# Wider weight pieces, later and earlier statistics, and one-pass transposes in a decoder trunk

## The chip, the cores and the metric

One core of one Trainium2 chip runs the whole program. The metric is device time of one launch in microseconds, the median of several runs; 1053.26 us for the kernel before, from 3 runs (1051.03 to 1053.49).

## The reference, cut to what matters

The input is `h` of 256 tokens x 1024, all in float32. Two layers, each a half-step SwiGLU feed-forward, a token mixer, and another half-step feed-forward; the mixer of the first layer is Mamba-2 (one chunk of 256 tokens, 32 heads in 4 groups), that of the second a sliding-window attention with sinks. A shared K/V projection stands between the layers.

```python
def rmsnorm(x, g):
    y = x * lax.rsqrt(jnp.mean(x * x, axis=-1, keepdims=True) + EPS)
    return y * g

def swiglu_half_step(h, g, w1, w3, w2):          # w1, w3: 1024 x 2816; w2: 2816 x 1024
    u = rmsnorm(h, g)
    return h + 0.5 * ((jax.nn.silu(u @ w1) * (u @ w3)) @ w2)

h = swiglu_half_step(h, ...)                     # layer 0, first FFN
h = h + mamba2_mixer(rmsnorm(h, ssm_norm), ...)  # ends in a grouped rmsnorm of y*silu(z), then @ w_out
h = swiglu_half_step(h, ...)
k, v = shared_kv(h, ...)
h = swiglu_half_step(h, ...)                     # layer 1
h = h + sliding_window_attention(rmsnorm(h, attn_norm), k, v, ...)
return swiglu_half_step(h, ...)                  # the last FFN
```

## The kernel before, in words

The residual stream lives transposed in SBUF: `hT` holds 8 tiles of 128 channels x 256 tokens. A matrix product in float32 is made from three products of float32r parts: a weight is cast to a high part `wh` by ScalarE and the rest `wl` is taken by VectorE (`Unit.part`, lines 165 to 169); activations have a high and a low part likewise (`vh`/`vl` from `Norm.split`, `uT` from `Norm.normalize`). From chunk 2 on (`up_wide`) one 512-column matmul does two of the three products.

**Weights.** A `Unit` (line 146) is 2048 columns of raw weights, fetched by SyncE into one of 3 buffers `raw`, and cut into 4 pieces of 512 columns; each piece is one cast and one subtraction. `wh` and `wl` are buffers of 1024 columns, 8 of each, so two pieces share a buffer and both wait until TensorE has read what was there. The raw buffer comes free, and SyncE issues the next fetch, when its last piece is subtracted.

**A feed-forward** (`run_ffn`, line 303) has 11 chunks of 256 hidden columns in two halves f. Each half is an up-projection (16 weight blocks), a `gate` (silu and product, split into parts) and the down-projection of an earlier half (`flush`). The rms factor does not stop it: the first chunks run on the unnormalised `vh`/`vl`, while `Norm.stats` computes 1/rms (`token_mean`: two float32 matmuls with a 1-column operand; an add on VectorE; a power on GpSimd) and `Norm.scale` spreads it over partitions (`spread`, line 228: two float32 matmuls of a broadcast column with the identity, and a copy). Then `normalize` writes `uT`. When these two steps stand in the instruction order is given as counts of matmuls: `later(n, fn)` runs `fn` once n more matmuls have been written.

**The last feed-forward** yields tokens on partitions, so its residual has to be transposed back: `residual` (line 412) adds `hT.T @ (2*identity)` into the four accumulators by 16 float32 matmuls, and the end multiplies by 0.5.

**Mamba** (`mamba`, line 476). `stage_a0` computes z and dt from unnormalised parts, with statistics and scale at 62 and 100 matmuls; `a_bc`, `a_x`, `a_z` are projections of group g with a convolution on VectorE; `stage_b` makes y of a group and its sum of squares `sq` (line 773); `stage_y(g, 30, 60)` places the group's statistics and its scaling (`y_stats`, `y_scale`) 30 and 60 matmuls later, beside the next group's projections; `stage_c`/`c_part` are the output projection.

**The opening** (lines 1125 to 1183) loads x in two halves (`xin`), transposes it by `turn_x(b)`, two channel tiles at a time, and casts the first weights piece by piece in a pinned order (`chained`, `behind`). `turn_x(2)` and `turn_x(3)` are called ahead of contraction steps 1 and 3 of the first up-projection.

**Order.** Each engine runs its queue in order. The order is laid out when the program is built, by a planner that goes by program order as priority and by its own estimates of what is ready; `tc.issue_after` pins an instruction behind another of its engine, `tc.high_priority` moves it ahead. Inside attention the matmul order is pinned (`strict`).

Of the kernel before, what the change touches and what calls it, by code (L numbers as in the profile page):

```python
# [11 lines left out]
F32 = mybir.dt.float32  # L12
F32R = mybir.dt.float32r
AF = mybir.ActivationFunctionType
ALU = mybir.AluOpType
# [3 lines left out]
P = 128  # L19
D = 1024  # L20
KT = D // P
S = 256
NT = S // P
# [17 lines left out]
def yoco_kernel(ctx: ExitStack, tc: tile.TileContext, a: dict, out: bass.AP):  # L41
    nc = tc.nc
# [11 lines left out]
    def bcast(src: bass.AP, n: int, off: int = 0, parts: int = P) -> bass.AP:  # L54
        return bass.AP(tensor=src.tensor, offset=src.offset + off, ap=[[0, parts], [1, n]])
# [21 lines left out]
    mean = const.tile([P, 2], F32, name="mean")  # L77
    nc.gpsimd.memset(mean[:, 0:1], 1.0 / D)
    nc.gpsimd.memset(mean[:, 1:2], 1.0 / 512.0)
    ident2 = const.tile([P, P], F32, name="ident2")  # L80
    nc.gpsimd.tensor_add(ident2, ident, ident)

    anti = const.tile([P, P], F32, name="anti")
    nc.gpsimd.memset(anti, 0.0)
    nc.gpsimd.affine_select(out=anti, in_=anti, pattern=[[1, P]], compare_op=ALU.not_equal, fill=1.0,
# [8 lines left out]
    def nm(s):  # L94
        uid[0] += 1
        return f"{s}_{uid[0]}"
# [5 lines left out]
    def in_turn(op, *args, **kw):  # L102
        if strict[0]:
            with tc.issue_after(pe[-1]):
                r = op(*args, **kw)  # L105
        else:
            r = op(*args, **kw)  # L107
        pe.append(r.ins)

    def mm(o, l, r, first, last):  # L110
        in_turn(nc.tensor.matmul, o, l, r, start=first, stop=last)
# [15 lines left out]
    def later(n, fn):  # L127
        soon.append((len(pe) + n, fn))
# [11 lines left out]
    def wmm3(o, wh, wl, uh, ul, first, last):  # L140
# [2 lines left out]
        mm(o, wl, uh, False, last)  # L143
        tick()

    class Unit:
        def __init__(self, parts, split=2, hold=False):
            n = 2048 // split
            raw = rawp.tile([P, 2048], F32, tag="raw", name=nm("raw"))
            for part in parts:  # L150
                if callable(part):
                    part()
                    continue
                lo, n0, shape, src, k0 = part
                nc.sync.dma_start(view(raw, shape, lo, n0)[:, k0:k0 + src.shape[1]], src)
            self.h, self.l = [], []
            self.raw, self.n = raw, n
            for i in range(split):
                self.h.append(whp.tile([P, n], F32R, tag="wh", name=nm("wh")))
                self.l.append(wlp.tile([P, n], F32R, tag="wl", name=nm("wl")))  # L160
            if not hold:
                for c in range(0, 2048, 512):
                    self.part(c)

        def part(self, c):
            rs = self.raw[:, c:c + 512]
            wh, wl = self.get(c, 512)
            return (nc.scalar.copy(wh, rs).ins,  # L168
                    nc.vector.tensor_sub(wl, rs, wh.bitcast(F32)).ins)  # L169

# [9 lines left out]
    def up_unit(w1, w3, c, half, cut=1, hold=False, between=None):  # L180
        cs = slice(c * 256, c * 256 + 256)
        n = 4 // cut
        parts = []
        for k in range(0, 4, n):
            r0 = half * 512 + k * P
            for i, w in enumerate((w1, w3)):
                parts.append((i * 256, 256, 512,
                              w[r0:r0 + n * P, cs].rearrange("(k p) c -> p k c", p=P), k))
            if between is not None and k == 0:
                parts.append(between)  # L190
        return Unit(parts, hold=hold)

    def row_unit(w, r0, hold=False):
        return Unit([(0, 1024, 1024, w[r0:r0 + 256, :].rearrange("(k p) c -> p k c", p=P), 0)], hold=hold)
# [33 lines left out]
    def spread(rs):  # L228
        pb = ps_tr.tile([P, S], F32, tag="tr", name=nm("pb"))
        for t in range(NT):  # L230
            mm(pb[:, t * P:(t + 1) * P], rs[:, t:t + 1].to_broadcast([P, P]), ident, True, True)
        rb = sb.tile([P, S], F32, tag="rsb", name=nm("rsb"), bufs=2)
        nc.vector.tensor_copy(rb, pb)
        return rb
# [68 lines left out]
    def run_ffn(layer, j, cur, nxt, hook=None, ups=None, at=(60, 84), pre=None):  # L303
# [5 lines left out]
        last = nxt is None  # L309
# [99 lines left out]
                for d in range(KT):  # L409
                    down(c, f, d, g)  # L410

        def residual():
            for t in range(NT):
                for n in range(2):
                    for i in range(4):
                        mm(acc[2 * t + n][:, i * P:(i + 1) * P], hT[:, 4 * n + i, t * P:(t + 1) * P],
                           ident2, False, False)

        pend = []

# [5 lines left out]
        slow = at[1] > 96  # L426
        for c in range(NCHUNK):
            for f in range(2):
                if c == 0 and f == 0:
                    later(*stats)  # L430
                    later(*scale)
                    with tc.issue_after(pe[-1]) if pe else nullcontext():
                        g0 = up_first()
                    if not slow:
                        start_gates()
                if c == 0:
                    continue
                pm = up(c, f)
                if slow and c == 1 and f == 0:
                    start_gates()  # L440
                g = gate(c, pm)
                if c < C:
                    if not (slow and c == 1 and f == 0):
                        flush(pend.pop(0))
                    if c == 1 and f == 1:
                        while pend:
                            flush(pend.pop(0))
                    pend.append((c, f, g))
                elif f == 0:
                    gc0 = g  # L450
                if c == 5 and len(gcols) == 1:
                    gain_cols(grow[1])
                if c == 5 and f == 0 and last:
                    residual()
                if c >= 3 and hook is not None:
                    next(hook, None)
        pend = pend[0]
# [9 lines left out]
        for t in range(NT):  # L467
            for n in range(2):
                down_t(C, 0, t, n, gc0)
                down_t(C, 1, t, n, g)  # L470
                cs = slice(n * 512, n * 512 + 512)
                o = sb.tile([P, 512], F32, tag="cv", name=nm("o"), bufs=2)
                nc.vector.tensor_scalar_mul(o, acc[2 * t + n], 0.5)
                nc.sync.dma_start(out[0, t * P:(t + 1) * P, cs], o)

    def mamba(mp, cur, nxt):
# [198 lines left out]
        def stage_a0():  # L675
            zs = mp.tile([P, 4, S], F32, tag="zs", name=nm("zs"), bufs=2)
            uz = [col_unit(w_in, [i * 256], 256) for i in range(2)]
            later(62, cur.stats)
            later(100, cur.scale)
            z0 = z_first(uz[0], ps_acc, "acc")  # L680
            dt_proj()
            z1 = z_first(uz[1], ps_mm, "mm")
            dt_scale()
            z_scale(z0, zs[:, 0:2, :])
            cur.normalize()
            z_scale(z1, zs[:, 2:4, :])
            a_bc(0)
            dt_soft()
            a_x(0)
            dt_cum()  # L690
            decay_rows(0)
            st[0] = st[0] + (zs,)
# [116 lines left out]
        def stage_y(g, n0, n1):  # L809
            later(n0, lambda: y_stats(g))  # L810
            later(n1, lambda: y_scale(g))
# [28 lines left out]
        stage_b(0)  # L840
        exps(1)
        for g in (2, 3):
            stage_y(g - 2, 30, 60)
            a_bc(g)
            prep(g - 1)
            a_x(g)
            a_z(g)
            stage_b(g - 1)
            exps(g)
            if g == 2:  # L850
                stage_c(0)
# [80 lines left out]
    def attention(ap, cur, kT, vtok, bias, nxt):  # L932
        snk = ap.tile([P, AH], F32, tag="snk", name="snk")
        nc.gpsimd.dma_start(snk, bcast(a["sinks"][0], AH))
        uq = [row_unit(a["w_q"][0], i * 256) for i in range(4)]
        qns, qTs = {}, {}

# [181 lines left out]
        for b in range(KT // 2):  # L1119
            for d in (2 * b, 2 * b + 1):  # L1120
                for k in range(4, KT):
# [6 lines left out]
    n0.open()  # L1128
    w13 = a["ffn_w1"][0, 0], a["ffn_w3"][0, 0]
    keep_warm(10)  # L1130
    ups = {0: [up_unit(*w13, 0, 0, 2, True,
                       lambda: nc.sync.dma_start(xin[:, :, 512:1024], xsrc[:, :, 512:1024]))]}
    ups[0].append(up_unit(*w13, 0, 1, 2, True))
    ups[1] = [up_unit(*w13, 1, h, 2, True) for h in range(2)]
# [6 lines left out]
    def turn_x(b):  # L1141
        pool, tag = ((ps_tr, "tr"), (ps_acc, "acc"), (ps_acc, "acc"), (ps_mm, "mm"))[b]
        px = pool.tile([P, 2, S], F32, tag=tag, name=nm("px"))
        for i in range(2):
            for t in range(NT):
                nc.tensor.transpose(px[:, i, t * P:(t + 1) * P],
                                    xin[:, t, (2 * b + i) * P:(2 * b + i + 1) * P], ident)
        if b == 0:
            gain_cols(grow[0])
        for i in range(2):  # L1150
            with behind(*(prev[-1] if prev else ())):
                n0.split(2 * b + i, px[:, i, :])
            with behind(*n0.last):
                prev.append(ups[0][b // 2].part((b % 2) * 1024 + i * 512))
        pxs.append(px)

    def keep_x():
# [17 lines left out]
        for b in (3, 0, 1, 2):  # L1175
# [3 lines left out]

    turn_x(0)  # L1180
    turn_x(1)
    run_ffn(0, 0, norms[0], norms[1], ups=ups, at=(128, 142),
            pre={1: lambda: turn_x(2), 3: lambda: turn_x(3), 7: keep_x})
    xpool.close()
    with tc.tile_pool(name="mp", bufs=1) as mp:
        mamba(mp, norms[1], norms[2])
# [45 lines left out]
```

## Time and profile before

| what | value |
|---|---|
| median of 3 runs | 1053.26 us (1051.03 to 1053.49) |
| the profiled execution, own time | 1054.95 us |
| its span, first to last instruction | 1053.2 us |
| mean granted TensorE clock | 0.995 |
| VectorE busy | 760.0 us (72%) |
| ScalarE busy | 628.1 us (60%) |
| DMA moved | 187.22 MB, mean 178 GB/s |

Busy time is the union of an engine's instructions. A matmul's record is longer than the time to the next one's start, since matmuls are pipelined: a row of the timeline that merges n matmuls gives the start of the first and the end of the last, so the pace is read from starts. "PEld" is the weight load of a matmul. The clock is the share of full speed that was granted to TensorE: 1.00 is 2.4 GHz, 0.50 is 1.2 GHz.

### The profile page before, as it was taken

The numbers are of one execution on the slowest core, as the hardware profiler recorded it, in microseconds if no ns is written. First come the engines' busy times: TensorE is split into PE (matmuls) and PEld (weight loads), VectorE is DVE, ScalarE is ACT, GpSimd is POOL, SyncE is SP. The second block draws the span as 40 slices with busy tenths as digits, with TensorE's granted clock in tenths as the row PEclk, the third lists the DMA queues.
The fourth block names the chain that finished last, engine by engine and source line by source line (L and its number), as shares of the span: only waits on it lengthen the run. The fifth ranks groups of instructions, "written<-read, shape, count | busy, mean of one in ns | idle before, by whom it ended". The sixth has DMA issues, their size and how long they took to land.

```text
span 1053.2 us, 18596 instructions
## 1 busy us (share of the span) xinstructions
PE 1037.4 (98%) x7130; PEld 950.7 (90%) x7130; DVE 760.0 (72%) x1564; ACT 628.1 (60%) x1348; POOL 54.5 (5%) x79
## 2 busy tenths in 40 slices
PE   8999999999999999999999999999999999999998
PEld 8999999989899999999999999999986699888886
DVE  6975756897899899756566976675677678564753
ACT  7664655677867656646456754465567566454652
POOL 1100000003210010000000000010002000000000
PEclk9999999999999999999999999999999999999999
DMA  8665657546456365556565556585641336464641
GB/s 287 210 223 172 207 174 215 173 129 204 135 169 225 133 173 192 180 181 203 171 224 160 191 173 200 163 284 173 222 160 41 120 122 212 154 225 129 217 142 41
DMA packets 138921, 187.22 MB, mean 178 GB/s; under 512 B 4940, under 2 KB 120816, under 8 KB 138832
## 3 DMA queue, kind: packets, MB, share of 16 engines
q1 hardware_dynamic: 136496, 179.32, 52.8%
q0 software_dynamic: 2288, 6.69, 2.2%
q8 instruction: 56, 0.92, 0.4%
q14 instruction: 33, 0.27, 0.1%
q10 hardware_dynamic: 48, 0.02, 0.0%
HBM read 184.90 MB, written 1.11 MB: 177 GB/s over the span
## 4 chain that ended last, share of the span: by engine, by line
PE 72%; issue 21%; DVE 4%; POOL 1%; DMA 1%; ACT 1%; SPq 0%; POOLq 0%; DVEq 0%; ACTq 0%
PE pm L107 37%; PE acc L107 18%; PE pa L107 5%; PE pp L107 5%; PE pq L105 2%; PE pa L105 1%; PE ps L105 1%; DVE wl L169 1%; PE py L107 1%; DVE sp L982 1%; PE po L105 1%; DMA xin<-in_x_dram 1%; PE pkv L107 1%; ACT em L607 1%; DVE zs L767 1%
## 5 line engine op out<-in xcount | busy, mean ns | idle before, releaser
L169 DVE TENSOR_TENSOR wl<-raw,wh 128x512 fp32r<-128x512 f32 x676 | 434.5, 685 | 54.0 <-ACT wh L168 41.5
L168 ACT CAST wh<-raw 128x512 fp32r<-128x512 f32 x676 | 375.6, 618 | 84.5 <-PE acc L107 32.1
L107 PE MATMUL pm<-uT,wh 128*128 128x512 f32 x1152 | 402.9, 392 | 0.0
L107 PE MATMUL pm<-uT,wl 128*128 128x256 f32 x1152 | 321.7, 280 | 0.0
L107 PEld LDWEIGHTS pm<-uT,wh 128*128 128x128 f32 x1152 | 216.1, 188 | 45.7 <-issue 0.2
L107 PEld LDWEIGHTS pm<-uT,wl 128*128 128x128 f32 x1152 | 216.5, 188 | 1.1 <-DVE wl L169 0.2
L107 PE MATMUL acc<-ghl,wh 128*128 128x256 f32 x1056 | 191.2, 282 | 0.0
L336 ACT COPY lo<-pm 128x256 f32<-128x256 f32 x144 | 53.3, 370 | 211.0 <-PE pm L107 211.0
L337 DVE TENSOR_TENSOR tp<-pm,lo 128x256 f32<-128x256 f32 x144 | 60.8, 422 | 154.4 <-ACT lo L336 154.4
L107 PEld LDWEIGHTS acc<-ghl,wh 128*128 128x128 f32 x1056 | 162.3, 188 | 2.7 <-ACT ghl L344 0.3
L107 PE MATMUL acc<-ghl,wl 128*128 128x256 f32 x528 | 148.3, 282 | 0.0
L107 PE MATMUL pp<-uT,wh 128*128 128x256 f32 x576 | 107.1, 287 | 2.2 <-ACT uT L300 1.4
L107 PEld LDWEIGHTS acc<-ghl,wl 128*128 128x128 f32 x528 | 99.4, 188 | 0.0
L107 PEld LDWEIGHTS pp<-uT,wh 128*128 128x128 f32 x576 | 90.4, 192 | 3.1 <-ACT uT L300 1.5
L107 PE MATMUL pp<-uT,wl 128*128 128x256 f32 x288 | 81.5, 284 | 0.0
L107 PE MATMUL pm<-vh,wh 128*128 128x256 f32 x256 | 73.2, 286 | 0.0
L107 PE MATMUL pm<-vl,wh 128*128 128x256 f32 x256 | 72.4, 283 | 0.0
L107 PE MATMUL pm<-vh,wl 128*128 128x256 f32 x256 | 72.3, 283 | 0.0
L107 PE MATMUL acc<-wh,ghl 128*128 128x512 f32 x176 | 58.3, 395 | 0.0
L107 PEld LDWEIGHTS pp<-uT,wl 128*128 128x128 f32 x288 | 55.1, 191 | 0.0
L344 ACT CAST ghl<-g 128x256 fp32r<-128x256 f32 x88 | 35.7, 406 | 31.6 <-DVE g L341 31.2
L345 DVE TENSOR_TENSOR ghl<-g,ghl 128x256 fp32r<-128x256 f32 x88 | 36.9, 420 | 17.5 <-ACT ghl L344 17.5
(234 smaller groups left out, 1275.5 us busy)
## 6 DMA issues: line engine op xcount, KB each, us to landing
raw<-in_ffn_w_dram SPq DMA_DIRECT2D x168, 512.0 KB, 4.8
raw<-in_ffn_w_dram SPq DMA_DIRECT2D x44, 1024.0 KB, 5.2
raw<-in_ssm_w_in_dram SPq DMA_DIRECT2D x16, 1024.0 KB, 5.4
raw<-in_ssm_w_out_dram SPq DMA_DIRECT2D x8, 1024.0 KB, 5.0
raw<-in_ffn_w_dram SPq DMA_DIRECT2D x16, 256.0 KB, 6.0
raw<-in_ssm_w_in_dram SPq DMA_DIRECT2D x8, 512.0 KB, 5.3
pr<-pdram POOLq DMA_DIRECT2D x8, 512.0 KB, 4.4
raw<-in_w_q_dram SPq DMA_DIRECT2D x4, 1024.0 KB, 4.9
```

The costliest lines, as they stand in the source:

```text
L105: r = op(*args, **kw)
L107: r = op(*args, **kw)
L168: return (nc.scalar.copy(wh, rs).ins, nc.vector.tensor_sub(wl, rs, wh.bitcast(F32)).ins)
L169: nc.vector.tensor_sub(wl, rs, wh.bitcast(F32)).ins)
L336: nc.scalar.copy(lo, pw[:, 256:512])
L337: nc.vector.tensor_add(o, pw[:, 0:256], lo)
L344: nc.scalar.copy(gh, g)
L345: nc.vector.tensor_sub(gl, g, gh.bitcast(F32))
L607: r = nc.scalar.activation(*args, **kw)
L767: nc.vector.tensor_mul(zs[:, j, :], y1, zs[:, j, :])
L982: chain[1] = op(*args, **kw).ins
```

## The change

A unit is cut into 2 pieces of 1024 columns, except in chunks 0 to 2 of the first feed-forward and in attention, where it stays at 512 (the opening's first two chunks call `part` themselves, at 512). `spread` uses transposes in place of float32 matmuls. The last residual is transposed into SBUF by `keep_rows`, four transposes in each of chunks 4 to 7 with a copy by ScalarE, and added in the last instruction of each output block. Statistics move: `stats` of the first feed-forward from 128 to 122 matmuls, `stage_a0` from 62 and 100 to 60 and 84, `stage_y` of groups 0 and 1 from 30 and 60 to 72 and 104. In the opening the first unit is fetched by 8 transfers in place of 4, and `turn_x(2)` is called at step 2 in place of 1.

```diff
-    ident2 = const.tile([P, P], F32, name="ident2")
-    nc.gpsimd.tensor_add(ident2, ident, ident)
...
+    grain = [1024]
...
-                for c in range(0, 2048, 512):
-                    self.part(c)
-        def part(self, c):
-            rs = self.raw[:, c:c + 512]
-            wh, wl = self.get(c, 512)
+                for c in range(0, 2048, grain[0]):
+                    self.part(c, grain[0])
+        def part(self, c, n=512):
+            rs = self.raw[:, c:c + n]
+            wh, wl = self.get(c, n)
             return (nc.scalar.copy(wh, rs).ins,
                     nc.vector.tensor_sub(wl, rs, wh.bitcast(F32)).ins)
...
     def spread(rs):
-            mm(pb[:, t * P:(t + 1) * P], rs[:, t:t + 1].to_broadcast([P, P]), ident, True, True)
+            in_turn(nc.tensor.transpose, pb[:, t * P:(t + 1) * P], rs[:, t:t + 1].to_broadcast([P, P]), ident)
...
-        def residual():
-            for t in range(NT):
-                for n in range(2):
-                    for i in range(4):
-                        mm(acc[2 * t + n][:, i * P:(i + 1) * P], hT[:, 4 * n + i, t * P:(t + 1) * P],
-                           ident2, False, False)
+        kept = []
+
+        def keep_rows(i):
+            if i == 0:
+                kept.append(sb.tile([P, NT, D], F32, tag="v", name=nm("rows"), bufs=2))
+            t, n = i // 2, i % 2
+            pr = ps_mm.tile([P, 512], F32, tag="mm", name=nm("pr"))
+            for d in range(4):
+                in_turn(nc.tensor.transpose, pr[:, d * P:(d + 1) * P],
+                        hT[:, 4 * n + d, t * P:(t + 1) * P], ident)
+            nc.scalar.copy(kept[0][:, t, n * 512:n * 512 + 512], pr)
...
         for c in range(NCHUNK):
             for f in range(2):
+                grain[0] = 512 if pre and c < 3 else 1024
...
-                if c == 5 and f == 0 and last:
-                    residual()
+                if 4 <= c < 8 and f == 0 and last:
+                    keep_rows(c - 4)
...
-                nc.vector.tensor_scalar_mul(o, acc[2 * t + n], 0.5)
+                nc.vector.scalar_tensor_tensor(out=o, in0=acc[2 * t + n], scalar=0.5,
+                                               in1=kept[0][:, t, cs], op0=ALU.mult, op1=ALU.add)
...
-            later(62, cur.stats)
-            later(100, cur.scale)
+            later(60, cur.stats)
+            later(84, cur.scale)
...
         for g in (2, 3):
-            stage_y(g - 2, 30, 60)
+            stage_y(g - 2, 72, 104)
...
     def attention(ap, cur, kT, vtok, bias, nxt):
+        grain[0] = 512
...
-    ups = {0: [up_unit(*w13, 0, 0, 2, True,
+    ups = {0: [up_unit(*w13, 0, 0, 4, True,
...
-    run_ffn(0, 0, norms[0], norms[1], ups=ups, at=(128, 142),
-            pre={1: lambda: turn_x(2), 3: lambda: turn_x(3), 7: keep_x})
+    run_ffn(0, 0, norms[0], norms[1], ups=ups, at=(122, 142),
+            pre={2: lambda: turn_x(2), 3: lambda: turn_x(3), 7: keep_x})
```

## Rows read from the trace of the kernel before

**Rows 1.** The page, part 1: busy us (share of the span) x instructions.
```profile
PE 1037.4 (98%) x7130; PEld 950.7 (90%) x7130; DVE 760.0 (72%) x1564; ACT 628.1 (60%) x1348; POOL 54.5 (5%) x79
```

**Rows 2.** The chain of waits, in a middle chunk: start us, us, what.
```profile
454.82 5.55 PE pm L107 x32
460.37 2.85 PE acc L107 x24
```

**Rows 3.** Waits of PE: who for whom: us in total, times, longest us.
```profile
PE px L1146 <- DMA xin<-in_x_dram: 1.9, 2, 1.6
PE pa L107 <- DVE wl L169: 1.8, 1, 1.8
PE pc L107 <- DVE sq L773: 1.5, 1, 1.5
PE pp L107 <- ACT uT L300: 1.4, 1, 1.4
PE pb L107 <- POOL rs L219: 1.0, 1, 1.0
```

**Rows 4.** Windows: stretch, us, busy us of each engine, granted clock, DMA.
```profile
216.10:219.40 3.30, 3.30 (x18) 3.30 (x17) 3.30 (x8) 3.10 (x5) 0.00 (x0) 0.50 0.02 5
...
311.70:315.00 3.30, 3.30 (x17) 3.30 (x17) 2.89 (x6) 3.30 (x11) 0.00 (x0) 0.50 0.00 0
```

**Rows 5.** Timeline of PE in the last feed-forward: start us, us, what.
```profile
950.50 3.73 PE L107 MATMUL acc<-ident,hT 128*128 128x128 f32 x32
953.99 0.48 PE L107 MATMUL pm<-uT,wh 128*128 128x512 f32 x1
```

**Rows 6.** Timeline of PE in Mamba: four transposes, then one spread.
```profile
244.14 0.60 PE L667 MATMUL ptx<-ident,xc 128*128 128x128 f32 x4
...
281.80 0.60 PE L107 MATMUL pb<-ident,grs 128*128 128x128 f32 x4
282.16 0.49 PE L107 MATMUL pp<-uT,wh 128*128 128x256 f32 x2
```

**Rows 7.** The transposes by their tile: duration ns min/median/max, first and last start.
```profile
L667 PE MATMUL ptx<-ident,xc x32: 272/273/421, 244.1 to 359.3; 128*128 128x128 f32 x32
```

**Rows 8.** Timeline of PE, statistics and spread of the first feed-forward.
```profile
24.79 0.50 PE L107 MATMUL pc<-mean,xsq 128*128 128x1 f32 x4
27.79 0.71 PE L107 MATMUL pb<-ident,rs 128*128 128x128 f32 x4 [0.96 <-POOL rs L219]
```

**Rows 9.** Timeline of POOL between those two.
```profile
25.91 0.56 POOL L483 DMA_DIRECT2D rows<-in_ssm_conv_w_dram  x1 [0.16 <-POOL rows L486]
...
26.99 0.75 POOL L219 TENSOR_TENSOR rs<-me,mhalf 128x2 f32<-128x2 f32 x1
```

**Rows 10.** Timeline of PE, statistics and spread at Mamba's start.
```profile
205.57 0.50 PE L107 MATMUL pc<-mean,sq 128*128 128x1 f32 x4
...
210.23 0.60 PE L107 MATMUL pb<-ident,rs 128*128 128x128 f32 x4
```

**Rows 11.** Timeline of POOL and DVE between and behind those two.
```profile
206.35 1.09 POOL L219 TENSOR_TENSOR rs<-me,mhalf 128x2 f32<-128x2 f32 x1 [174.96 <-DVE me L217]
...
210.61 0.69 DVE L169 TENSOR_TENSOR wl<-raw,wh 128x512 fp32r<-128x512 f32 x1 [2.54 <-ACT wh L168]
211.22 0.42 DVE L233 COPY rsb<-pb 128x256 f32<-128x256 f32 x1
```

**Rows 12.** Groups by line and shape: busy us, mean ns of one, idle before.
```profile
L169 DVE TENSOR_TENSOR wl<-raw,wh 128x512 fp32r<-128x512 f32 x676 | 434.5, 685 | 54.0 <-ACT wh L168 41.5 <-PE pm L107 11.7
...
L168 ACT CAST wh<-raw 128x512 fp32r<-128x512 f32 x676 | 375.6, 618 | 84.5 <-PE acc L107 32.1 <-PE pp L107 12.4 <-DMA raw<-in_ffn_w_dram 11.0
...
L345 DVE TENSOR_TENSOR ghl<-g,ghl 128x256 fp32r<-128x256 f32 x88 | 36.9, 420 | 17.5 <-ACT ghl L344 17.5
L344 ACT CAST ghl<-g 128x256 fp32r<-128x256 f32 x88 | 35.7, 406 | 31.6 <-DVE g L341 31.2
```

**Rows 13.** Windows: one stretch of Mamba, columns as in rows 4.
```profile
284.00:309.00 25.00, 25.00 (x220) 24.43 (x219) 24.11 (x46) 16.59 (x32) 3.06 (x4) 1.00 0.55 168
```

## The prediction

> **What bounds the kernel now.** I read the page's busy times first: TensorE is busy for 98% of the span and no other engine is near it [rows 1]. That figure alone says little, since a matmul's record is longer than its pace, so the chain of waits comes next. In a middle chunk of a feed-forward it shows nothing but matmuls: 32 of the up-projection in 5.55 us, 24 of the down-projection in 2.85 us, with no other engine between them [rows 2]. 24 matmuls of 256 columns in 2.85 us are 0.119 us each, the pace of all dense parts; there VectorE and ScalarE have slack and only fewer or shorter matmuls help. The list of what TensorE waited for is then short enough to go through entry by entry: five entries of 1 us or more, 7.6 us together [rows 3]. Three of them, one wait each (ScalarE's uT at Mamba's start, VectorE's sq of group 0, VectorE's wl of the first output projection) are followed by a stretch in which the windows show a granted clock of 0.50, the 1.2 GHz level, with TensorE full of work (the first and the last of the three stand in [rows 4]); each covers 3.30 us in which half the work was done, so it costs another 1.65 us. A wait of 1.4 to 1.8 us there is worth 3.1 to 3.5 us.
>
> So the kernel is a stream of matmuls with some 7 us of waits, 5 us of half clock, and float32 side work on top. The change touches all three.
>
> **The change part by part.** Sums go against the profiled execution, 1054.95 us by its own time (1053.2 us of span and 1.75 us around it, which nothing here touches); it lies 1.7 us above the median of the runs, and I carry the difference over to the median.
>
> *The residual.* Gone are 16 float32 matmuls, 32 instructions on TensorE, from 950.50 to 953.99: 3.49 us, 0.109 us each [rows 5]. Added are 16 transposes in four blocks. Four transposes of Mamba span 0.60 us from the first start to the end of the last, whose record is 0.273 us [rows 6, 7]: four begin within 0.33 us, a pace of 0.11 us. A block costs between 0.33 and 0.60 us; I take 0.45 us, since the matmul behind it can hide little of its weight load, and four make 1.8 us. Gain 1.7 us (1.1 to 2.2). The four copies of 512 columns go to ScalarE, 0.62 us each by the cast's row [rows 12]; they lie beside 8.4 us of matmuls per half chunk (the two pieces of rows 2), and the PSUM buffer that a block takes is needed again one half later. If that cover went, each would cost its 0.62 us, 2.5 us in all; queued behind them on ScalarE are casts and the next gate. The last instruction of each output block reads one operand more and keeps its shape: nothing.
>
> A rule of the Trainium skill speaks against this part and the next: its page "TensorE: Matmul & The Clock Gate", section "Part 4: PE-mode transpose", puts a transpose at about 275 ns inside a kernel. The trace agrees with it as the length of one record, 0.273 us, but not as the pace; with it as the pace, the rival of slow transposes below would be the forecast.
>
> *The spread.* Nine are made: five for norms, four for groups. One takes 282.16 - 281.80 = 0.36 us in four instructions [rows 6]; two transposes at 0.11 us, one of them partly behind the matmul ahead, take 0.14 us. Gain 0.22 us each, 2.0 us in all (from 0, if a transpose paces as a pair of today's, to 2.2 us).
>
> *First feed-forward.* TensorE waits 0.96 us at the spread; 2.20 us pass from the statistics (24.79 us) to the start of the power (26.99 us), because GpSimd first issues two fetches of Mamba's small weights, whose buffers were waiting for the statistics too [rows 8, 9]. All of that moves along when the statistics move up by two blocks of three matmuls (the count runs in threes: 129 becomes 123), 6 x 0.119 = 0.7 us. The wait falls to 0.25 us. Gain 0.7 us (0 to 0.96).
>
> *Mamba's start.* Statistics now come after 60 matmuls in place of 63, the spread at 86 in place of 101 (counts again in threes): 15 matmuls, 1.8 us earlier. Is the factor ready? From statistics to the end of the power takes 206.35 + 1.09 - 205.57 = 1.87 us [rows 10, 11]; the new distance is the statistics and 24 matmuls, over 2.86 us: yes. The copy rsb, which today stands behind a weight piece that VectorE idled 2.54 us for [rows 11], can go in that idle time. So uT of the first block comes at least 1.8 us earlier, and the 1.4 us wait goes; the half-clock stretch behind it goes with it, 3.05 us in all. What is late next: `normalize` needs VectorE for about 1.5 us a block (two operations of 256 columns and one of 512, 0.42 and 0.69 us by rows of like shape [rows 12]), and TensorE at full clock uses a block in six matmuls, 0.71 us; today the half clock hides this. I take 0.5 us off. Gain 2.6 us (1.0 to 3.3). The four casts, the dt chain and the next groups' fetches, which hang on these buffers, move up with it.
>
> *Statistics of groups 0 and 1.* pc of group 0 stands 30 matmuls behind stage b and waits 1.5 us for sq [rows 3]; 42 matmuls later is 5 us later, so sq has long been there. With the half-clock stretch the gain is 3.1 us. Moved along are four matmuls, the add, GpSimd's power (nothing is queued behind it until the next group's masks), the spread, and per tile a scaling, a cast and a subtraction; they are first read by an output projection behind the next stage b. Gain 3.1 us (0 if VectorE is the bound behind it; below).
>
> *Wide pieces.* A cast of 512 columns takes 618 ns, one of 256 takes 406: 0.83 ns a column and 194 ns fixed. Subtractions, 685 and 420 ns: 1.03 ns a column and 155 ns fixed [rows 12]. No row has 1024 columns: by the slopes 1.04 and 1.21 us. From above, a pair could cost its two old durations, 1.24 and 1.37 us, no saving; from below it loses the whole fixed part, some 300 pairs x 0.155 = 47 us of VectorE, none of it on the path in the feed-forwards. But a piece is ready later: today the first half of a buffer after 0.62 + 0.69 = 1.31 us, then after 2.25 us, the whole buffer 0.26 us later than now. In feed-forwards TensorE waited for no weight at all: the one wl in its list is Mamba's [rows 3]. In Mamba VectorE is full (24.11 of 25.00 us in 284 to 309 us [rows 13]), and the 1.8 us wait for wl sits right behind. Less fixed work helps there, 0.95 us of delay hurts, and the planner lays the queues out anew. I take a loss of 1.0 us, bounds a gain of 3.45 us (the wl wait and its stretch go) and a loss of 6 us (two new waits like today's).
>
> *The opening.* Two waits for x sum to 1.9 us [rows 3]. With one step of weights in front of the second half of x in place of two, 0.25 MB less is ahead of it, and its transposes are no longer due ahead of step 1. But SyncE issues four transfers more, and VectorE's chain of small pieces sets the pace soon after. Gain 0.5 us (from a loss of as much, if the later weights lag, to the longest of these waits, 1.6 us).
>
> Sum: -1.7 - 2.0 - 0.7 - 2.6 - 3.1 + 1.0 - 0.5 = -9.6 us; 1054.95 becomes 1045.35, and the median 1053.26 becomes 1043.7 us.
>
> **The rivals.** *VectorE takes back Mamba's gains.* It is full from 284 to 309 us [rows 13], and if it decides when the output projection starts, the 2.6 and 3.1 us reappear as a longer wait for wl. Against it: each pair made one spares it 0.155 us there. Then -1.7 - 2.0 - 0.7 - 0.5 = -4.9: 1048.4 us. *The wait for wl goes too*, because VectorE saves the fixed part of every second piece and starves less behind stalled statistics: -3.45 us and no loss of 1.0: 1039.2 us. *Slow transposes*, at the pace of their record, 0.273 us [rows 7]: 34 take 9.3 us against 3.49 + 9 x 0.36 = 6.7 us removed, a loss of 2.6 us where the forecast gains 3.7: 1050.0 us. Against it: the four of [rows 6]. *The planner's new layout opens one wait of Mamba's kind* on top of the first rival: 1048.4 + 3.1 = 1051.5 us. *Slower:* wide pieces arrive late in Mamba, whose 28 units (20 of w_in, 8 of w_out) go through a VectorE that is nearly full; each late first piece stalls TensorE 0.95 us. The other parts gain 10.6 us, so it decides from 12 late units; with 15 of 28 it gives 1053.3 - 10.6 + 14.3 = 1057.0 us. Against it: one wait for wl stands in the list now.
>
> **How the numbers follow.** Chances: forecast 0.45 (own range 1041.5 to 1046.5), VectorE takes back 0.20, wl goes too 0.20, new layout 0.07, late pieces 0.05, slow transposes 0.03. A measurement tells 0.3%, 3.2 us, from no change. Faster than 1050.1 us: forecast, the first two rivals and most of the slow transposes, 0.87; the same: 0.08; slower: 0.05. The range 1038.5 to 1050.0 leaves out the last cases and the far end of the wl case.
>
> **What would show it.** Right: no wait for sq, uT or rs of 1 us in TensorE's list; at most one stretch at clock 0.50 after the opening; 16 transposes in blocks of about 0.45 us; spreads of 0.14 us; feed-forward pieces still 5.55 and 2.85 us. Wrong: TensorE waits for wl in several places of Mamba, gate or copy waits inside feed-forwards, or new half-clock stretches.

## The result and the profile after

The changed kernel takes 1043.84 us (median of 4 runs, 1043.33 to 1044.65) against 1053.06 us, a ratio of 0.9917 with an interval of 0.9900 to 0.9934. A second time, beside the experiments, it took 1043.36 us (6 runs, 1043.23 to 1044.72), a ratio of 0.9901 (0.9885 to 0.9917). The forecast was 1043.7 us. The total is right; several of its terms are not, and their errors cancel. The profiled execution took 1044.65 us by its own time, with a span of 1042.9 us. One execution of the kernel before, beside the last experiments, took 3586.76 us and is counted nowhere.

First the page of the changed kernel: busy times.

```profile
PE 1031.1 (99%) x7096; PEld 942.7 (90%) x7096; DVE 738.8 (71%) x1260; ACT 605.6 (58%) x1048; POOL 56.1 (5%) x78
```

TensorE issues 34 matmuls fewer (7130 in [rows 1]). The three half-clock stretches of the profile before [rows 4] have no successor. The page's clock row in 40 slices can't tell, since it reads 9 in every slice before as after; windows around the three places do (columns as in [rows 4]):

```profile
214.00:220.00 6.00, 5.91 (x47) 5.42 (x46) 6.00 (x14) 3.58 (x6) 0.00 (x0) 1.00 0.12 36
276.00:282.00 6.00, 5.33 (x46) 5.13 (x46) 5.18 (x10) 5.44 (x11) 0.71 (x1) 1.00 0.80 314
302.00:308.00 6.00, 6.00 (x54) 5.83 (x50) 6.00 (x9) 4.08 (x11) 3.16 (x5) 1.00 0.87 264
```

Next, what TensorE waited for (us in total, times, longest), to be held against [rows 3].

```profile
PE acc L104 <- DVE ghl L344: 1.4, 2, 0.8
...
PE px L1153 <- DMA xin<-in_x_dram: 1.1, 1, 1.1
PE pm L104 <- DVE tp L326: 0.8, 1, 0.8
...
PE ptx L673 <- DVE xdt L676: 0.7, 1, 0.7
PE ptx L673 <- ACT cbs L664: 0.7, 1, 0.7
```

The waits for wl, sq, uT and rs are gone. New are two waits for a gate inside feed-forwards (ghl), which the prediction had named as a sign against it, one for tp behind the first feed-forward's normalization, and two small ones in Mamba. To see where the gain lies I took the start of landmark matmuls from both traces:

| first or last matmul of | before, us | after, us | shift |
|---|---|---|---|
| first feed-forward: pm, first | 8.59 | 8.86 | +0.27 |
| its acc, first | 34.45 | 33.80 | -0.65 |
| its acc, last | 197.74 | 199.42 | +1.68 |
| Mamba: pp, first | 214.98 | 214.93 | -0.05 |
| output projection of group 0: pa, first | 306.74 | 302.17 | -4.57 |
| the same, last | 321.70 | 313.54 | -8.16 |
| second feed-forward: pm, first | 397.00 | 388.89 | -8.11 |
| third feed-forward: acc, last | 777.00 | 769.82 | -7.18 |
| last feed-forward: acc, first | 877.97 | 870.17 | -7.80 |
| its acc, last | 1048.41 | 1038.79 | -9.62 |

The first feed-forward loses 2.3 us between its first and last acc, Mamba gains 9.8 from there to the end of the first output projection, the second and third feed-forward lose 0.9, the last one gains 1.8. Of the 9.8 us, 5.0 are the three half-clock stretches of the one execution profiled before (1.65 us each, by the estimate of the prediction). The residual and the spread are as forecast. This is TensorE's timeline around one block of the moved residual and around one spread (start, us, what):

```profile
926.01 0.60 PE L104 MATMUL pr<-ident,hT 128*128 128x128 f32 x4
926.36 0.48 PE L104 MATMUL pm<-uT,wh 128*128 128x512 f32 x1
...
282.86 0.38 PE L104 MATMUL pb<-ident,grs 128*128 128x128 f32 x2
283.00 0.48 PE L104 MATMUL pp<-uT,wh 128*128 128x256 f32 x2
```

Four transposes take 0.35 us up to the next matmul, a spread 0.14 us (0.36 in [rows 6]). All nine spreads, each read from its start to the next matmul's start, sum to 1.43 us, where they took 3.46 before. The record of one transpose is still 0.27 us; the pace is a third of it. And the chain of waits in a middle chunk answers to [rows 2] without a difference:

```profile
446.48 5.55 PE pm L104 x32
452.03 2.85 PE acc L104 x24
```

The groups of the subtraction and of the cast (busy us, mean ns, idle before), for [rows 12]:

```profile
L168 DVE TENSOR_TENSOR wl<-raw,wh 128x1024 fp32r<-128x1024 f32 (+1 forms) x372 | 411.7, 1129 | 82.2 <-ACT wh L167 80.5
L167 ACT CAST wh<-raw 128x1024 fp32r<-128x1024 f32 (+1 forms) x372 | 347.1, 970 | 108.7 <-PE acc L104 44.7
```

372 pairs in place of 676 save VectorE 22.8 us of busy time and ScalarE 28.5. What that is worth, and why it hurts in a feed-forward, VectorE's timeline ahead of the new gate wait at 572.52 us shows:

```profile
568.31 1.22 DVE L168 TENSOR_TENSOR wl<-raw,wh 128x1024 fp32r<-128x1024 f32 x1
569.44 0.42 DVE L340 TENSOR_TENSOR g<-tp,sl 128x256 f32<-128x256 f32 x1
569.77 2.35 DVE L168 TENSOR_TENSOR wl<-raw,wh 128x1024 fp32r<-128x1024 f32 x2
572.04 0.42 DVE L344 TENSOR_TENSOR ghl<-g,ghl 128x256 fp32r<-128x256 f32 x1
```

Two pieces of 1.22 us stand in VectorE's queue between the gate's product and its split, which TensorE needs; the split starts when they are through. The page "VectorE: DVE Perf Modes" of the Trainium skill, section "The TRN2 errata — SBUF-src ops pay a fixed extra latency per instruction", gives (N+151)/0.96 ns for a float32 `tensor_tensor` add, measured at 512 and 2048 columns; an estimate by it for the subtraction of 1024 columns is 1.224 us, and the trace agrees (1.22 us). Its advice, that one large tile pays the fixed part once and many small ones each time, holds for VectorE's busy time (22.8 us less); for the kernel's time it decides nothing by itself, as the second experiment shows.

### The profile page after: what moved, and what is told of

Its sections match the earlier page's. It is cut to its first block, busy times and chain, and to the rows that moved or that the text cites. A ratio compares the mean times of both kernels' runs of the same rounds, so it can differ in the third digit from the quotient of the medians.

```text
span 1042.9 us, 17921 instructions
## 1 busy us (share of the span) xinstructions
PE 1031.1 (99%) x7096; PEld 942.7 (90%) x7096; DVE 738.8 (71%) x1260; ACT 605.6 (58%) x1048; POOL 56.1 (5%) x78
## 4 chain that ended last, share of the span: by engine, by line
PE 68%; issue 21%; DVE 5%; DMA 2%; POOL 2%; ACT 1%; SPq 0%; POOLq 0%; DVEq 0%; ACTq 0%
PE pm L104 36%; PE acc L104 17%; PE pa L104 5%; PE pp L104 3%; DVE wl L168 2%; PE pq L102 2%; PE pa L102 1%; PE ps L102 1%; PE po L102 1%; DVE sp L989 1%; DMA xin<-in_x_dram 1%; DMA raw<-in_ssm_w_out_dram 1%; PE pkv L104 1%; PE py L104 1%; DMA raw<-in_ssm_w_in_dram 1%
## 5 line engine op out<-in xcount | busy, mean ns | idle before, releaser
L168 DVE TENSOR_TENSOR wl<-raw,wh 128x1024 fp32r<-128x1024 f32 (+1 forms) x372 | 411.7, 1129 | 82.2 <-ACT wh L167 80.5
L167 ACT CAST wh<-raw 128x1024 fp32r<-128x1024 f32 (+1 forms) x372 | 347.1, 970 | 108.7 <-PE acc L104 44.7
L104 PE MATMUL pp<-uT,wh 128*128 128x256 f32 x576 | 104.9, 283 | 0.1
```

Source lines behind the costliest of these rows:

```text
L167: return (nc.scalar.copy(wh, rs).ins, nc.vector.tensor_sub(wl, rs, wh.bitcast(F32)).ins)
```

## The experiments

Eleven other kernels and the changed one again, 4 to 12 runs each. Medians from different chips differ a little for the same kernel (1043.84 and 1043.36 above); ratios are to the kernel before on the same chip. Unless said otherwise the edit is made in the changed kernel.

**All pieces at 512 columns again.**

```diff
-    grain = [1024]
+    grain = [512]
...
-                grain[0] = 512 if pre and c < 3 else 1024
+                grain[0] = 512
```

> The changed kernel with all weight pieces at 512 columns again; every other part of the change stays. Theory A (the 1024-column pieces relieve VectorE in Mamba and took away the wait for wl at the first output projection with the half-clock stretch behind it, and they caused the waits for the gate at the ends of the first two feed-forwards): the gate waits go (about -1.4 us), the wl wait and its stretch come back (+3.45 us), so about 1045.9 us. Rival B (the moved statistics took the wl wait away; the wide pieces only cost): the gate waits go and nothing comes back, about 1042.4 us. The changed kernel is at 1043.84 us.

Measured: 1046.06 us (1044.22 to 1046.93), ratio 0.9921 (0.9903 to 0.9939). What TensorE waited for:

```profile
PE pa L104 <- DVE wl L168: 1.7, 2, 1.5
...
PE pp L104 <- DVE cv L636: 0.9, 1, 0.9
```

No gate wait is left and the wl wait is back: theory A, and its number. By the medians of two chips the wide pieces are worth 2.2 us here, where the forecast had a loss of 1.0. Much of that is clock: the two executions at a granted clock of 1.00 take 1044.22 and 1044.49 us, the four at 0.997 and 0.998 take 1045.94 to 1046.93.

**Wide pieces alone**, in the kernel before, with the change's own choice of 512 columns in the first chunks and in attention.

```diff
+    grain = [1024]
...
-                for c in range(0, 2048, 512):
-                    self.part(c)
+                for c in range(0, 2048, grain[0]):
+                    self.part(c, grain[0])
...
+                grain[0] = 512 if pre and c < 3 else 1024
...
+        grain[0] = 512
```

> The kernel before with the wide pieces as its only change. Theory A: the wl wait and its stretch go (-3.45 us), the gate waits come (+1.4 us): about 1051.0 us against 1053.06. Rival B (wide pieces only cost): the wl wait of 1.8 us stays, the gate waits come, about 1054.5 us. The waits for sq and uT in Mamba and for rs in the first feed-forward stay under both.

Measured: 1054.70 us (12 runs, 1053.00 to 1056.30), ratio 1.0007 (0.9994 to 1.0019). What TensorE waited for:

```profile
PE pp L107 <- ACT uT L302: 1.8, 1, 1.8
PE pa L107 <- DVE wl L171: 1.8, 1, 1.8
...
PE pc L107 <- DVE sq L776: 1.6, 1, 1.6
PE acc L107 <- DVE ghl L347: 1.4, 2, 0.8
```

Theory A falls for the pieces by themselves: the wl wait stays and the gate waits come, as rival B had it. Together with the first experiment this means that the wl wait goes only with the pieces *and* another part of the change.

**Wide pieces in Mamba alone.**

```diff
-                grain[0] = 512 if pre and c < 3 else 1024
+                grain[0] = 512
...
     def mamba(mp, cur, nxt):
+        grain[0] = 1024
```

> The changed kernel with 1024-column pieces in Mamba alone; all feed-forwards and attention use 512. Theory A: the gate waits at the ends of feed-forwards one and two (0.60 and 0.82 us) go and Mamba keeps its gain: about 1042.4 us. Rival: the gate waits come from the new order of the work and stay, or Mamba starts worse because VectorE brings more work over from the first feed-forward: about 1043.8 us or more.

Measured: 1041.94 us (1041.83 to 1042.05), ratio 0.9883 (0.9864 to 0.9902). TensorE's waits for a gate and for tp:

```profile
PE acc L104 <- DVE ghl L344: 0.6, 1, 0.6
...
PE pm L104 <- DVE tp L326: 0.2, 1, 0.2
```

The gate wait of the second feed-forward is gone. The one of the first stays at 194.55 us, because the pieces that stand ahead of that gate are already Mamba's first.

**The opening as before.**

```diff
-    ups = {0: [up_unit(*w13, 0, 0, 4, True,
+    ups = {0: [up_unit(*w13, 0, 0, 2, True,
...
-            pre={2: lambda: turn_x(2), 3: lambda: turn_x(3), 7: keep_x})
+            pre={1: lambda: turn_x(2), 3: lambda: turn_x(3), 7: keep_x})
```

> The changed kernel with the opening as before: two blocks of small pieces, the second half of x due after the first step of weights. Theory C (two further blocks of quarter pieces shift VectorE's and ScalarE's queues, so that a later cast waits for its DMA with the tokens' cast queued behind it, and TensorE waits 0.81 us for tp at 40.48): this wait goes and the first matmul is 0.27 us earlier, about 1042.7 us; the waits for x return by at most 0.4 us. Rival D (the 0.81 us come from the statistics moved up, or from the wide pieces): 1043.6 us or above, with the wait in place.

Measured: 1043.95 us (1043.16 to 1045.20), ratio 0.9904 (0.9886 to 0.9922). The wait for tp is not in the list, that for x is 2.1 us in place of 1.1. By the median it is nothing. Theory C isn't shown: the same wait for tp measures 1.6, 0.5 and 0.4 us in three other executions with the new opening (the two experiments on Mamba's statistics below, and the changed kernel's second profile) and is in no list of two more (the spread's experiment and the one on the first feed-forward's statistics). The wait for x scatters as much: 0.3 to 2.0 us in the executions with the new opening. In the first profile of the changed kernel ScalarE had waited 0.95 us for a transfer of weights at 36.22 us, with a cast of uT queued behind it, and VectorE waited 0.81 us for that cast with tp queued behind its subtraction; so I take the wait to move with that transfer. This was not tried.

**The spread by float32 matmuls again.**

```diff
-            in_turn(nc.tensor.transpose, pb[:, t * P:(t + 1) * P], rs[:, t:t + 1].to_broadcast([P, P]), ident)
+            mm(pb[:, t * P:(t + 1) * P], rs[:, t:t + 1].to_broadcast([P, P]), ident, True, True)
```

> The changed kernel with the float32 matmul spread back (two instructions a tile at the row's pace of 0.11 us each in place of one transpose). By the prediction's term the nine spreads cost 0.36 us in place of 0.14 us: +2.0 us, about 1045.8 us against 1043.84. Rival: the spread stands beside a wait that absorbs it, as in Mamba, and only the five of the norms show: +1.1 us, 1044.9 us.

Measured: 1046.60 us (1045.84 to 1046.99), ratio 0.9933 (0.9914 to 0.9952). TensorE's timeline at the same spread as above:

```profile
281.89 0.61 PE L104 MATMUL pb<-ident,grs 128*128 128x128 f32 x4
282.25 0.48 PE L104 MATMUL pp<-uT,wh 128*128 128x256 f32 x2
```

0.36 us again. The nine sum to 3.68 us in place of 1.43: 2.2 us, near the forecast's term of 2.0. From the first pm to the end of the span it is 1036.25 us in place of 1034.09, the same 2.2 us; against the changed kernel's second profile (1033.33) it is 2.9, so the whole span is good to some 0.7 us.

**The residual by float32 matmuls again.**

```diff
...
-                if 4 <= c < 8 and f == 0 and last:
-                    keep_rows(c - 4)
+                if c == 5 and f == 0 and last:
+                    residual()
...
```

> The changed kernel with the last residual back as 16 float32 matmuls on a doubled identity, no transposes and no copies. By the prediction's term: +1.7 us (the stage of the trace says +1.8), about 1045.6 us. Rival: the copies on ScalarE or the longer last instruction cost something that the trace hides elsewhere, and undoing shows less than +1.1 us.

Measured: 1046.22 us (1044.69 to 1047.45), ratio 0.9930 (0.9912 to 0.9948). TensorE's timeline:

```profile
940.88 3.73 PE L107 MATMUL acc<-ident,hT 128*128 128x128 f32 x32
944.36 0.48 PE L107 MATMUL pm<-uT,wh 128*128 128x512 f32 x1
```

The 3.48 us are back, and the last feed-forward from its first pm to its last acc takes 188.34 us in place of 186.52. 1.8 us, so a block of four transposes costs 0.42 us (the forecast's 0.45); its copies show nowhere.

**The statistics of groups 0 and 1 at their old places.**

```diff
-            stage_y(g - 2, 72, 104)
+            stage_y(g - 2, 30, 60)
```

> The changed kernel with the statistics of groups 0 and 1 back at 30 and 60 matmuls behind stage b. By the prediction's term the wait for sq (1.5 us) returns and, in executions where the clock falls behind it, 1.65 us more: 1045.3 to 1046.9 us. Rival: VectorE, relieved by the wide pieces, has sq ready in time and nothing returns: 1043.8 us.

Measured: 1045.01 us (1044.12 to 1045.44), ratio 0.9917 (0.9896 to 0.9938). Two of TensorE's waits:

```profile
PE pm L104 <- DVE tp L326: 1.6, 1, 1.6
...
PE pc L104 <- DVE sq L779: 0.6, 1, 0.6
```

Between the two: sq is late by 0.6 us where it was late by 1.5 in [rows 3], and no half-clock stretch follows in this execution. Of the 3.1 us forecast, the medians show 1.2 (1.7 against the second median, from another chip), but the 1.6 us wait for tp in this execution lies in the first feed-forward, which the edit doesn't touch. From the last acc of the first feed-forward to the first pm of the second, which leaves that wait out, this trace takes 189.91 us, the two of the changed kernel 189.47 and 189.11: 0.4 to 0.8 us.

**Mamba's first statistics at their old places.**

```diff
-            later(60, cur.stats)
-            later(84, cur.scale)
+            later(62, cur.stats)
+            later(100, cur.scale)
```

> The changed kernel with Mamba's first statistics back at 62 and 100. By the prediction's term uT is late again by 1.4 us with a possible stretch at half clock: 1045.2 to 1047.2 us, the first pp about 1 to 1.8 us later. Rival: the factor's wait is hidden by the planner's other order (pz ahead of pc), and nothing returns: 1043.8 us.

Measured: 1048.49 us (1047.93 to 1049.32), ratio 0.9953 (0.9936 to 0.9970). TensorE's waits:

```profile
PE pa L104 <- DVE wl L168: 1.8, 1, 1.8
PE pp L104 <- ACT uT L299: 1.8, 1, 1.8
```

More than either side expected: 4.7 us. uT is late again, and so is wl, some 90 us further on, although the pieces are wide.

**Mamba's statistics and wide pieces, nothing else**, in the kernel before: the second experiment's edit, and with it the edit just above the other way round (62 and 100 become 60 and 84).

> The kernel before with the wide pieces and Mamba's first statistics at 60 and 84; nothing else of the change. Theory of the pair (the wait for wl at the first output projection goes only where VectorE both starts Mamba earlier and has fewer pieces): uT (1.8 us) and wl (1.8 us) go together, sq stays at 1.6 us: 3.3 to 4.7 us below the kernel with wide pieces alone, so 1050.0 to 1051.4 us. Rival: the wl wait goes only with the later statistics of groups 0 and 1: uT goes alone, about 1052.9 us.

Measured: 1048.49 us (1048.21 to 1050.16), ratio 0.9951 (0.9934 to 0.9968). What TensorE waited for has neither uT nor wl; sq is down:

```profile
PE pb L107 <- POOL rs L221: 1.0, 1, 1.0
...
PE pc L107 <- DVE sq L776: 0.6, 1, 0.6
```

The theory of the pair holds, by more than its number: 6.2 us below the wide pieces alone, 5.9 by the two ratios.

**The first feed-forward's statistics back.**

```diff
-    run_ffn(0, 0, norms[0], norms[1], ups=ups, at=(122, 142),
+    run_ffn(0, 0, norms[0], norms[1], ups=ups, at=(128, 142),
```

> The changed kernel with the first feed-forward's statistics back at 128 matmuls. By the prediction's term the wait for rs returns with 0.7 us: about 1044.5 us. Rival: the wait for tp behind it (0.81 us in the changed kernel) takes the difference up, since the same casts and transfers set its end: 1043.8 us.

Measured: 1043.83 us (1043.54 to 1044.31) against 1043.36 of the changed kernel on the same chip. TensorE's timeline at the spread:

```profile
27.80 0.43 PE L104 MATMUL pb<-ident,rs 128*128 128x128 f32 x2 [0.72 <-POOL rs L218]
```

The wait is back with the forecast's 0.7 us, and the rival is right all the same: this trace has no wait for tp, and its last acc of the first feed-forward comes 0.33 us later than in the changed kernel's second trace, as much as its first pm does. The moved statistics hand their gain to the next wait.

**A version to beat both.**

```diff
-                grain[0] = 512 if pre and c < 3 else 1024
+                grain[0] = 512
...
     def mamba(mp, cur, nxt):
+        grain[0] = 512
...
             uz = [col_unit(w_in, [i * 256], 256) for i in range(2)]
+            grain[0] = 1024
```

> Both kernels to beat: the changed kernel with 512-column pieces in all feed-forwards, attention and Mamba's first two units (z of group 0), 1024 in the rest of Mamba. Theory: five wide subtractions of 1.22 us stand ahead of the gate at the end of the first feed-forward when only Mamba is wide; with the first four halved the wait of 0.60 us for the gate there falls to 0.1 us or less: about 1041.4 us against 1041.94 of the kernel with all of Mamba wide. Rival: the pieces for z at 512 bring VectorE's load at Mamba's start up by 4 x 0.155 us and uT later: 1042 us or more.

> The changed kernel itself, beside the version above on one chip: 1043.8 us, and executions with the granted clock at 1.0 of the span.

Measured: 1041.13 us (1040.54 to 1041.41), ratio 0.9876 (0.9859 to 0.9893); the changed kernel on the same chip 1043.36. VectorE's timeline at the end of the first feed-forward:

```profile
191.48 1.83 DVE L168 TENSOR_TENSOR wl<-raw,wh 128x512 fp32r<-128x512 f32 x2
193.22 0.42 DVE L344 TENSOR_TENSOR ghl<-g,ghl 128x256 fp32r<-128x256 f32 x1
193.56 1.22 DVE L168 TENSOR_TENSOR wl<-raw,wh 128x1024 fp32r<-128x1024 f32 x1
```

Two short pieces are ahead of the gate, the first wide one behind it, and no gate wait is in the list any more. The 2.2 us over the changed kernel are shown on one chip; the 0.8 us over the kernel with all of Mamba wide lie between two chips.

## Why the prediction was right, and where it was not

The signs that the prediction named for being right are all there: no wait of 1 us for sq, uT or rs, no half-clock stretch, spreads of 0.14 us, feed-forward pieces of 5.55 and 2.85 us. One sign of being wrong is there too, the waits for a gate.

**Right by its steps: spread and residual.** -2.0 and -1.7 us were forecast, -2.2 and -1.8 are what the traces show when each is undone. The page "TensorE: Matmul & The Clock Gate" of the Trainium skill, section "Part 4: PE-mode transpose", has about 275 ns for a bf16 transpose in one kernel's context; the trace agrees with that as the length of the record (0.27 us), not as the pace (0.35 us for four, up to the next matmul).

**Mamba's start, and wide pieces: one mechanism, priced as two.** The forecast gave -2.6 and +1.0. What it missed is that the two act together on the first output projection, 90 us later, through the order of VectorE's queue there. The first block of the projection reads 256 columns of each of four buffers of 1024 columns, two of either weight unit, so it can't end without the second unit. In the kernel before, VectorE's timeline reads:

```profile
301.99 2.49 DVE L169 TENSOR_TENSOR wl<-raw,wh 128x512 fp32r<-128x512 f32 x4
...
308.45 2.19 DVE L767 TENSOR_TENSOR zs<-y,zs 128x256 f32<-128x256 f32 x2
310.57 1.28 DVE L169 TENSOR_TENSOR wl<-raw,wh 128x512 fp32r<-128x512 f32 x2
```

and in the kernel after:

```profile
297.75 2.35 DVE L168 TENSOR_TENSOR wl<-raw,wh 128x1024 fp32r<-128x1024 f32 x2
300.30 0.48 DVE L771 SCALAR_TENSOR_TENSOR y<-xc,cols,py 128x256 f32<-128x256 f32 x1 [0.20 <-PE py L104]
...
303.89 2.20 DVE L773 TENSOR_TENSOR zs<-y,zs 128x256 f32<-128x256 f32 x2
306.01 1.21 DVE L168 TENSOR_TENSOR wl<-raw,wh 128x1024 fp32r<-128x1024 f32 x1
```

Before, the second unit's pieces stand behind the products y and zs of the last stage b and begin at 310.57 us, 3.8 us after the projection's first matmul (306.74); TensorE stops. After, the last of the four wide pieces that the block reads stand ahead of y; VectorE is through with them in time to wait 0.20 us for TensorE's product, and the piece at 306.01 is for later. With only one of the two edits a part of the second unit is behind zs again: one wide piece at 308.11 us where the statistics went back, one at 311.35 with the wide pieces alone, three short ones from 305.58 with the short pieces. Neither the earlier start (short pieces: wl waits 1.5 us) nor the shorter work (wide pieces alone: 1.8 us) is enough; the two without the rest of the change are. That they act together is shown by these runs: the pieces lose 0.7 us alone and are worth 2.2 with the rest present. That the order in this queue passes it on is read from the traces, and why the planner lays out another order with both was not looked into. The earlier statistics alone, in the kernel before, were not tried either. "The wait for wl goes too" was a rival with 0.20. Its wait did go, and its two reasons, fewer fixed parts and a VectorE that starves less behind stalled statistics, are close to the two edits of the pair; its 1039.2 us did not come, because other terms of the sum were too large.

**Statistics of groups 0 and 1: over-sized.** -3.1 forecast, -1.2 by the medians and -0.4 to -0.8 within Mamba by the traces. With the pair above, sq is late by only 0.6 us at the old place (both kernels that keep it beside the pair, by the fences above), and no half clock follows in either trace. The sum took part of the same lateness away twice.

**First feed-forward and opening: -0.7 and -0.5 forecast, nothing shown.** The wait for rs is gone, and the next wait, for tp, takes the gain up. The prediction asked "what is late next" for Mamba and not here.

**Gate waits: not in the sum.** The term for wide pieces looked at when the *weights* are ready, half a buffer 0.95 us later. It didn't ask what else is queued behind a piece: the gate's split. This costs 0.60 and 0.82 us.

**The clock: counted as if it always fell.** The forecast gave two waits 1.65 us each for the stretch at half clock behind them [rows 4]. In the second experiment waits of 1.6 to 1.8 us stand in the same three places, and its windows (columns as in [rows 4]) show the full clock behind them, here at the first and the third:

```profile
216.00:222.00 6.00, 3.62 (x24) 2.84 (x23) 5.93 (x14) 4.11 (x6) 0.00 (x0) 1.00 0.41 127
...
311.00:317.00 6.00, 4.38 (x37) 4.38 (x38) 5.11 (x9) 5.54 (x14) 0.00 (x0) 1.00 0.62 198
```

Its one half-clock stretch lies in the opening instead, at 9 to 12 us. The executions of the kernel before beside the experiments, sorted by granted clock over the span, show how much the clock varies:

| granted clock | executions | us |
|---|---|---|
| 0.999, 1.0 | 6 | 1050.98 to 1051.47 |
| 0.997, 0.998 | 15 | 1051.59 to 1054.23 |
| 0.995, 0.996 | 14 | 1054.00 to 1056.07 |
| 0.993 | 3 | 1056.75 to 1056.88 |

The profile on which the forecast rests is from the third line (0.995). At full clock the median before is 1051.3 us and after 1043.6 (its ten executions all have 0.999 or 1.0): 7.7 us from work and waits, where the forecast had 9.6 - 3.3 = 6.3. The other 1.5 us of the 9.2 are clock, where it had 3.3. The parts add up to about the 7.7: at a granted clock of 0.999 or 1.0 the pair alone takes 1048.2 to 1048.6 us (four executions), 3.0 under the 1051.3; with 2.2 for the spreads, 1.8 for the residual and 0.4 to 0.8 for the statistics of groups 0 and 1 that is 7.4 to 7.8. Carrying the profile's distance to the median over, 1.7 us, happened to be about the price of one stretch.

So the forecast is right in direction and in its two arithmetic parts; the total is right because two errors cancel. By the medians, the terms for the statistics of groups 0 and 1, the first feed-forward and the opening were 1.9 + 0.7 + 0.5 = 3.1 us too large. The pair of Mamba's start and wide pieces was forecast with -2.6 + 1.0 = -1.6 us and brought 5.2 by itself (0.0049 of 1053), gate waits included: 3.6 us more. Of the 5.2, some 2.2 are clock. That a total 0.1 us off came of this is luck. The prediction also counted five waits of 1 us or more; the list holds a sixth, 1.1 us for the constant `dummy` at the start, which is in both kernels, so no term hangs on it.

## What to carry to other kernels

Where one engine is full over a whole stage, edits at the stage's start and edits that shorten its work are not summed but tried together: here the wait at the end went with both and with neither alone. When instructions are merged into longer ones, look at what else stands in that engine's queue behind them: merge where the engine is the bound, and leave short pieces where it only has to answer quickly. Before pricing a clock stretch seen in one profile, look at how many executions have it.

## What the runs showed of the hardware

Waits of 1.4 to 1.8 us between dense matmuls are followed by 3.3 us at 1.2 GHz in the trace of the kernel before, and waits of 1.6 to 1.8 us at the same three places by none in the trace with wide pieces alone. 32 of 38 executions of the kernel before have less than 0.999 of the clock, none of ten of the kernel after, whose longest wait after the opening is 0.8 us. That this is due to the shorter waits is not shown: the kernel with the old residual has no longer wait after the opening in its trace, and three of its six executions have 0.998. The Trainium skill's page "TensorE: Matmul & The Clock Gate", in "Part 1: The HAM clock gate (the "warmup" mystery)", says of a kernel's start that the same kernel runs a different number of matmuls at the slow clock from run to run; the table shows the like over the whole span. What decides in a single execution stays open: only the clock's mean is known for executions without a trace.
